# Same-chunk tables of a state-space layer, expanded in DRAM before they are loaded

## The chip, the core and the metric

The kernel runs on one core of one Trainium2 chip. The metric is the device time of one execution in microseconds (us), the median of the runs. The core has TensorE (PE, with its weight loads as PEld), VectorE (DVE), ScalarE (ACT), GpSimd (POOL) and SyncE (SP); 16 DMA engines move data between DRAM and SBUF, for whichever engine issued the transfer.

## What is computed

A trunk of two layers over 256 tokens of 2048 features, all in float32: a convolution module, a feed-forward layer, a state-space module with a gated output, a second feed-forward layer, each added to `x`, and a last norm. The state-space module is the part that the change touches:

```python
u = h.reshape(bsz, L, 128, 16)                  # 128 groups of 16 channels
bu = einsum("blgc,gpc->blgp", u, bb)            # complex, 64 states per group
s = scan(s_t = a * s_{t-1} + bu_t)              # over the 256 tokens
y = Re(einsum("blgp,gcp->blgc", s, c)) + d_skip * h
z = gelu(y) @ w_glu                             # 2048 x 4096
out = z[:, :2048] * sigmoid(z[:, 2048:])
def mlp(h, w_up, w_down):                       # 2048 x 8192 and back
    a = relu(h @ w_up)
    return (a * a) @ w_down
```

## The kernel before

**Stages.** The weights stream from DRAM once, in steps of 1 MB (`raw`, three buffers; the convolution's first steps are smaller). ACT and DVE (for some steps POOL) split every half step into two float32r parts `hi` and `lo` (L117, L119; four buffers each), and PE multiplies them (L194 and L195, L215 to L217). SP issues all loads of `raw` and of the tables in one queue, in program order (`fetch`, L91). The first feed-forward layer is eight slices of `up` and `down`; its last two `down` slices are where the tables of the state-space layer begin to be loaded, by hooks that stand at single steps.

**The state-space layer.** The 256 tokens are cut into 32 chunks of 8. For each block `B` of 32 groups there are three tables of 2 MB, each 128 partitions by 32 groups by 128 floats: `W` takes a chunk's inputs to states (`ssm_front`), `M` takes a chunk's inputs to the outputs of the same chunk (`ssm_local`), `V` takes the state at a chunk's start to its outputs (`ssm_carry`). Between front and carry stand a transposition (`ssm_turn`) and the scan over chunks on DVE (`ssm_scan`, which also reads a 512 KB table `R`); after carry come gelu and the transposed, split output `yT` (`ssm_out`), which the gated product reads. `begin` does blocks 0 and 1 and the front of block 2; the rest is woven into the first eight steps of the gated product by the table `todo`, whose key is the step and its half: the front of block 3 at (1, 1), local of block 2 at (2, 0), its carry and the scan of block 3 at (2, 1), its `ssm_out` at (3, 0), local and carry of block 3 at (3, 1) and (5, 0). Steps 0 and 1 read `yT` of block 0, steps 2 and 3 of block 1, and so on.

**Where the tables come from.** They are computed in the background of the convolution's output product and of the first feed-forward layer: `ssm_prep` fills a list of pieces with a cost each, and `pop_bg` works them off at 2.75 units for each half step. `vstage(k)`, k = 0 to 15, makes `V` for eight groups and writes it to DRAM as `Vd`; `kstage(k)` multiplies it with the input matrix and writes a band of 16 by 15 blocks for each group as `Kd` (64 DMAs of 16 KB, POOL queue). Rows of `M` are shifted windows of that band: the rows of token d within the chunk (16 partitions) are columns 16 d to 16 d + 127 of it. So `table("M", B)` reads `Kd` with eight DMAs, one for each d, each into 16 partitions, in pieces of 128 floats (512 bytes); `W`, `V` and `R` are read with 128 partitions at a time, 8 KB to the row (4 KB for `R`).

**Order.** SP's queue is the program's order: `M` of block 0 is fetched ahead of a `raw` of the first feed-forward layer, `M` of block 1 in `begin`, `M` and `V` of blocks 2 and 3 ahead of the loads of steps 4 and 6 (`before_load`), with `R` of block 3 ahead of step 5. A table waits for a free one of six 16 KB buffers (`blk`). On PE, ACT, DVE and POOL a scheduler sets the order when the program is built.

Of the kernel before, what the change touches and what calls it, by code (L numbers as in the profile page):

```python
# [9 lines left out]
F32 = mybir.dt.float32  # L10
# [8 lines left out]
P = 128  # L19
# [8 lines left out]
G, ST, GC = 128, 64, 16  # L28
CH = 8
VW = PAD + T + 2  # L30
NQ = 4
# [5 lines left out]
class Trunk:  # L37
# [41 lines left out]
    def add(self, view, shape, consume, pre=None):  # L79
        self.steps.append((view, shape, consume, pre))  # L80
# [743 lines left out]
    def ssm_prep(self):  # L824
        nc, a, bg = self.nc, self.a, self.bg
        add = lambda c, fn: bg.append((c, fn))
        const = self.const
        self.Wd = self.dram.tile([P, G, P], F32, name="Wd")
        self.Kd = self.dram.tile([G, GC, 15 * GC], F32, name="Kd")
        self.Vd = self.dram.tile([P, G, P], F32, name="Vd")  # L830
        self.Bd = self.dram.tile([G, 2, ST, GC], F32, name="Bd")
        self.Rd = self.dram.tile([P, NQ, 1024], F32, name="Rd")
        self.xs = self.dram.tile([T, D], F32, name="xs")
        dma = nc.gpsimd.dma_start
# [221 lines left out]
        def vstage(k):  # L1056
            vs = s["bv"][:, 1, 0:1152].rearrange("p (g d c) -> p g d c", d=9, c=GC)
            g = slice(8 * k, 8 * k + 8)
            c = [s["c12"][:, i, g, :].unsqueeze(2).broadcast_to([P, 8, 8, GC]) for i in range(2)]
            p = [s[x][:, g, :].unsqueeze(3).broadcast_to([P, 8, 8, GC]) for x in ("pr", "pi")]  # L1060
            t = self.t4([P, 8, 8, GC], name="vt")
            v = vs[:, :, 1:9, :]
            self.tt(v, c[0], p[0], ALU.mult)
            self.tt(t, c[1], p[1], ALU.mult)
            self.tt(v, v, t, ALU.add)
            nc.scalar.activation(vs[:, :, 0, :], s["c12"][:, 0, g, :], AF.Copy)
            dma(out=self.Vd[:, g, :], in_=v.rearrange("p g d c -> p g (d c)"))

        def kstage(k):
            vs = s["bv"][:, 1, 0:1152].rearrange("p (g x) -> p g x", x=9 * GC)  # L1070
            bs = s["bv"].rearrange("p i x -> p (i x)")
            ps = self.bank([P, 2, P], name="kp")
            for gl in range(8):
                q, hh = gl % 4, gl // 4
                nc.tensor.matmul(ps[32 * q:32 * q + 32, hh, :], lhsT=bs[:, (8 * k + gl) * GC:(8 * k + gl + 2) * GC],
                                 rhs=vs[:, gl, 0:P], start=hh == 0, stop=hh == 1, skip_group_check=True)
            ks = self.t2([P, 2, P], name="ks")
            nc.scalar.activation(ks, ps, AF.Copy)
            for j in range(2):
                self.stt(ks[:, j, 0:GC], self.m32[:, 0:GC], self.dgl[:, k, j:j + 1], ks[:, j, 0:GC], ALU.mult, ALU.add)  # L1080
            kd = self.Kd.rearrange("(k h q) c e -> k q c h e", k=16, h=2, q=4)
            for q in range(NQ):
                dma(out=kd[k, q, :, :, 7 * GC:15 * GC], in_=ks[32 * q:32 * q + GC])
        for k in range(16):
            add(12, lambda k=k: vstage(k))
            add(5, lambda k=k: kstage(k))


    def ssm_slice(self, n):
# [46 lines left out]
    def table(self, kind, B):  # L1136

        if kind == "R":
            t = self.t4([P, 2, 16, 32], name="R") if B != 2 else self.S[:, 1]
            self.fetch(t.rearrange("p i g j -> p (i g j)"), self.Rd[:, B])  # L1140
        else:
            t = self.blk_tile([P, 32, P], name=kind + "t")
        if kind in "WV":
            src = self.Wd if kind == "W" else self.Vd
            for h in range(0, 32, 16):
                self.fetch(t[:, h:h + 16, :], src[:, 32 * B + h:32 * B + h + 16, :])
        elif kind == "M":
            base = self.Kd[32 * B:32 * B + 32]
            for d in range(CH):
                self.fetch(t[d * GC:(d + 1) * GC], base[:, :, d * GC:d * GC + P].rearrange("g c x -> c g x"))  # L1150
        self.tables[kind, B] = t

    def ssm_block(self, b):
# [306 lines left out]
```

## Time and profile before

| | us |
|---|---|
| median of 3 runs | 2077.03 (2071.52 to 2077.48) |
| profiled execution, its own time | 2073.18 |
| its span, first to last instruction | 2071.4 |
| PE busy | 1996.2 (96%) |
| DVE busy | 1426.4 (69%) |
| ACT busy | 942.6 (46%) |
| POOL busy | 304.4 (15%) |
| `Mt<-Kd`, 32 DMAs of 256 KB, median to landing | 14.1 |
| `Wt<-Wd`, 8 DMAs of 1 MB, median to landing | 9.8 |
| `Vt<-Vd`, 8 DMAs of 1 MB, median to landing | 12.3 |

[...] Times in rows are counted from the span's start. The state-space layer lies at about 1083 to 1206 us, the first feed-forward layer ahead of it, the second behind it.

### The profile page before, as it was taken

The page shows a single profiled execution, that of the slowest core. Times are in us where ns is not written, and L with a number is a line of the kernel's source. Part 1 is how long each engine was busy: PE and PEld are TensorE (multiplying, and loading weights), DVE is VectorE, ACT ScalarE, POOL GpSimd, SP SyncE. Part 2 cuts the span into 40 slices and gives each one's busy share as a digit, 9 for nine tenths or more (in the row PEclk, how much of TensorE's full clock was granted, in tenths as well). Part 3 has the DMA queues.
Part 4 walks back from the last instruction along what each step waited for, and adds up shares of the span by engine and source line. Part 5 has one row for each costly group of instructions (what it writes and reads, how often), then busy time and mean ns, then how long its engine had stood idle before and what let it go on. Part 6 is the DMA issues. An engine that isn't in the chain of part 4 may idle for free.

```text
span 2071.4 us, 28883 instructions
## 1 busy us (share of the span) xinstructions
PE 1996.2 (96%) x11612; PEld 1696.8 (82%) x11612; DVE 1426.4 (69%) x1897; ACT 942.6 (46%) x1155; POOL 304.4 (15%) x234
## 2 busy tenths in 40 slices
PE   8999798999999999999987799999999999999998
PEld 8899587788888888888876588888888888888887
DVE  7999899966767777776548635566565555655555
ACT  5444454454444545444433244455344444544444
POOL 2987401100000211111013410000000000000000
PEclk9999999999999999999997999999999999999999
DMA  8667367766856876667999975666566566565663
GB/s 230 164 176 209 108 201 246 229 216 189 266 185 188 220 217 214 202 213 225 254 299 222 216 234 184 192 184 193 184 189 197 183 189 197 183 211 192 186 192 133
DMA packets 330485, 420.09 MB, mean 203 GB/s; under 512 B 10081, under 2 KB 228241, under 8 KB 327889
## 3 DMA queue, kind: packets, MB, share of 16 engines
q1 hardware_dynamic: 316864, 384.86, 62.8%
q0 software_dynamic: 9488, 29.02, 4.7%
q10 hardware_dynamic: 4000, 4.38, 0.7%
q8 instruction: 91, 1.49, 0.3%
q14 instruction: 42, 0.34, 0.0%
HBM read 391.69 MB, written 26.53 MB: 202 GB/s over the span
## 4 chain that ended last, share of the span: by engine, by line
PE 79%; DVE 12%; DMA 4%; SPq 1%; issue 1%; ACT 1%; POOL 1%; ACTq 0%; POOLq 0%; DVEq 0%
PE acc L194 22%; PE acc L215 14%; PE acc L216 14%; PE acc L217 14%; PE acc L195 11%; DVE cv L792 6%; DMA raw<-in_ssm_w_glu_dram 2%; DVE lo L119 1%; SPq L91 1%; DVE vT L426 1%; DVE ws L783 1%; DMA raw<-in_mlp_w_down_dram 1%; DMA Vt<-Vd 0%; PE acc L204 0%; PE acc L205 0%
## 5 line engine op out<-in xcount | busy, mean ns | idle before, releaser
L117 ACT ACTIVATE hi<-raw 128x1024 fp32r<-128x1024 f32 x672 | 711.0, 1060 | 983.7 <-PE acc L217 480.0
L119 DVE TENSOR_TENSOR lo<-raw,hi 128x1024 fp32r<-128x1024 f32 x596 | 729.3, 1224 | 534.5 <-ACT hi L117 533.5
L194 PE MATMUL acc<-hT,hi 128*128 128x512 f32 x2048 | 726.5, 399 | 3.4 <-DVE t L771 3.4
L195 PE MATMUL acc<-hT,lo 128*128 128x256 f32 x2048 | 575.3, 281 | 3.3 <-DVE lo L119 3.3
L194 PEld LDWEIGHTS acc<-hT,hi 128*128 128x128 f32 x2048 | 385.3, 188 | 100.0 <-issue 3.2
L215 PE MATMUL acc<-hi,rT 128*128 128x512 f32 x992 | 388.6, 392 | 6.2 <-ACT hi L117 6.2
L195 PEld LDWEIGHTS acc<-hT,lo 128*128 128x128 f32 x2048 | 387.5, 189 | 4.8 <-DVE lo L119 3.9
L216 PE MATMUL acc<-lo,rT 128*128 128x512 f32 x992 | 387.4, 391 | 0.5 <-DVE lo L119 0.5
L217 PE MATMUL acc<-hi,rT 128*128 128x512 f32 x992 | 387.0, 390 | 0.0
L215 PEld LDWEIGHTS acc<-hi,rT 128*128 128x128 f32 x992 | 186.8, 188 | 47.2 <-ACT hi L117 6.6
L217 PEld LDWEIGHTS acc<-hi,rT 128*128 128x128 f32 x992 | 186.8, 188 | 39.5
L216 PEld LDWEIGHTS acc<-lo,rT 128*128 128x128 f32 x992 | 186.7, 188 | 39.0 <-DVE lo L119 1.0
L119 POOL TENSOR_TENSOR lo<-raw,hi 128x1024 fp32r<-128x1024 f32 x76 | 187.3, 2482 | 115.4 <-ACT hi L117 106.6
L204 PE MATMUL acc<-hT,hi 128*128 128x256 f32 x512 | 146.0, 285 | 1.5 <-ACT hi L117 1.5
L206 PE MATMUL acc<-hT,lo 128*128 128x256 f32 x512 | 145.4, 284 | 1.9 <-POOL lo L119 1.9
L205 PE MATMUL acc<-hT,hi 128*128 128x256 f32 x512 | 146.1, 286 | 0.2 <-DVE hT L252 0.2
L792 DVE SCALAR_TENSOR_TENSOR cv<-vT,dw,cv 128x256 f32<-128x256 f32 x348 | 142.1, 478 | 0.8
L217 PE MATMUL acc<-hi,yT 128*128 128x512 f32 x256 | 101.3, 396 | 8.1 <-DVE yT L231 8.1
L783 DVE TENSOR_TENSOR x<-x,acc 128x1024 f32<-128x1024 f32 (+1 forms) x72 | 83.6, 1161 | 33.3 <-PE acc L217 22.9
L204 PEld LDWEIGHTS acc<-hT,hi 128*128 128x128 f32 x512 | 98.5, 192 | 4.1 <-ACT hi L117 2.1
L215 PE MATMUL acc<-hi,yT 128*128 128x512 f32 x256 | 101.6, 397 | 0.0
L206 PEld LDWEIGHTS acc<-hT,lo 128*128 128x128 f32 x512 | 98.5, 192 | 3.0 <-POOL lo L119 2.1
(264 smaller groups left out, 1759.1 us busy)
## 6 DMA issues: line engine op xcount, KB each, us to landing
raw<-in_mlp_w_up_dram SPq DMA_DIRECT2D x128, 1024.0 KB, 5.8
raw<-in_mlp_w_down_dram SPq DMA_DIRECT2D x128, 1024.0 KB, 5.2
raw<-in_ssm_w_glu_dram SPq DMA_DIRECT2D x32, 1024.0 KB, 5.6
raw<-in_conv_w_in_dram SPq DMA_DIRECT2D x60, 512.0 KB, 5.5
raw<-in_conv_w_out_dram SPq DMA_DIRECT2D x16, 1024.0 KB, 5.3
Vd<-bv POOLq DMA_DIRECT2D x16, 512.0 KB, 5.0
Wt<-Wd SPq DMA_DIRECT2D x8, 1024.0 KB, 9.8
Mt<-Kd SPq DMA_DIRECT2D x32, 256.0 KB, 14.1
```

What stands on the lines that cost most here:

```text
L117: self.nc.scalar.activation(hi, sl, AF.Copy)
L119: ins = eng.tensor_tensor(out=lo, in0=sl, in1=hi.bitcast(F32), op=ALU.subtract)
L194: mm(accs[m], lhsT=hi[:, kk, c], rhs=x, start=first and kk == 0, stop=False)
L195: mm(accs[m][:, 0:T], lhsT=lo[:, kk, c], rhs=x[:, 0, :], start=False, stop=last and kk == 3)
L204: mm(accs[m], lhsT=hi[:, kk, c], rhs=x[:, 0, :], start=first and kk == 0, stop=False)
L205: mm(accs[m], lhsT=hi[:, kk, c], rhs=x[:, 1, :], start=False, stop=False)
L206: mm(accs[m], lhsT=lo[:, kk, c], rhs=x[:, 0, :], start=False, stop=last and kk == 3)
L215: mm(acc[:, b, :], lhsT=ak[:, 0, t], rhs=hi[:, kk, :], start=first and kk == 0, stop=False)
L216: mm(acc[:, b, :], lhsT=ak[:, 0, t], rhs=lo[:, kk, :], start=False, stop=False)
L217: self.mm_last = mm(acc[:, b, :], lhsT=ak[:, 1, t], rhs=hi[:, kk, :], start=False, stop=last and kk == 1)
L783: self.nc.vector.tensor_tensor(out=out, in0=a, in1=b, op=op)
L792: return self.nc.vector.scalar_tensor_tensor(out=out, in0=a, scalar=s, in1=b, op0=op0, op1=op1)
```

## The change

A DRAM tensor `Md` of the shape of `Wd` and `Vd` is added. Thirty-two DMAs on POOL's queue copy the windows of `Kd` into it, DRAM to DRAM, 256 KB each (`mstage(B, d)`: 16 by 32 pieces of 512 bytes). They are listed behind `kstage`, from k = 4 on, for the block that is then complete. To hold the list's pace, `kstage` is entered at 4 and later 3 units instead of 5, an `mstage` at 0.5. `table("M", B)` then reads `Md` as `W` and `V` are read: two DMAs of 1 MB, 128 partitions, 8 KB to the row.

```diff
+        self.Md = self.dram.tile([P, G, P], F32, name="Md")
...
+        def mstage(B, d):
+            dma(out=self.Md[d * GC:(d + 1) * GC, 32 * B:32 * B + 32, :],
+                in_=self.Kd[32 * B:32 * B + 32, :, d * GC:d * GC + P].rearrange("g c x -> c g x"))
         for k in range(16):
             add(12, lambda k=k: vstage(k))
-            add(5, lambda k=k: kstage(k))
+            add(4 if k < 4 else 3, lambda k=k: kstage(k))
+            if k >= 4:
+                for d in range(2 * (k % 4), 2 * (k % 4) + 2):
+                    add(0.5, lambda B=k // 4 - 1, d=d: mstage(B, d))
+        for d in range(CH):
+            add(0.5, lambda d=d: mstage(NQ - 1, d))
...
-        if kind in "WV":
-            src = self.Wd if kind == "W" else self.Vd
+            src = {"W": self.Wd, "M": self.Md, "V": self.Vd}[kind]
             for h in range(0, 32, 16):
                 self.fetch(t[:, h:h + 16, :], src[:, 32 * B + h:32 * B + h + 16, :])
-        elif kind == "M":
-            base = self.Kd[32 * B:32 * B + 32]
-            for d in range(CH):
-                self.fetch(t[d * GC:(d + 1) * GC], base[:, :, d * GC:d * GC + P].rearrange("g c x -> c g x"))
```

SP's queue from the end of the first feed-forward layer to step 6 of the gated product (`raw` are weights, `xJ` the layer's input, the other names the tables), as one piece of the difference:

```order
 L91 DMA Wt<-Wd 128x2048 x2
 L91 DMA xJ<-xs 32x8x128 x4
-L91 DMA Mt<-Kd 16x32x128 x8
+L91 DMA Mt<-Md 128x2048 x2
 L91 DMA Vt<-Vd 128x2048 x2
 L91 DMA Wt<-Wd 128x2048 x2
 L91 DMA raw<-in_ssm_w_glu_dram 128x4x512
-L91 DMA Mt<-Kd 16x32x128 x8
+L91 DMA Mt<-Md 128x2048 x2
 L91 DMA Vt<-Vd 128x2048 x2
 L91 DMA raw<-in_ssm_w_glu_dram 128x4x512
 L91 DMA R<-Rd 128x1024
```

No transfer changes its place; each group of eight `M` loads is two, and `V`, `raw` and `R` stand behind them as before.

POOL's queue around k = 3 to 5 before (`bv` is `vstage`'s result, `ks` that of one `kstage`):

```order
L1083 DMA Kd_2991<-ks_7140 16x2x128 x4
L1067 DMA Vd_2992<-bv_6554 128x8x128
L1083 DMA Kd_2991<-ks_7301 16x2x128 x4
L1067 DMA Vd_2992<-bv_6554 128x8x128 x2
L1083 DMA Kd_2991<-ks_7469 16x2x128 x4
```

and the same place of the changed kernel:

```order
L1084 DMA Kd_2991<-ks_7124 16x2x128 x4
L1068 DMA Vd_2993<-bv_6555 128x8x128
L1087 DMA Md_2992<-Kd_2991 16x32x128 x8
L1084 DMA Kd_2991<-ks_7282 16x2x128 x4
L1068 DMA Vd_2993<-bv_6555 128x8x128
L1084 DMA Kd_2991<-ks_7421 16x2x128 x4
```

The eight copies of a block, which the list has in pairs, stand in one burst ahead of the `Kd` writes of k = 4, 8 and 12, and those of the last block behind k = 15. The first of each burst waits for the `Kd` writes of the step just ahead of it.

## Rows read from the trace of the kernel before

**Rows 1.** The chain that ended last, shares of the span by engine.
```profile
PE 79%; DVE 12%; DMA 4%; SPq 1%; issue 1%; ACT 1%; POOL 1%; ACTq 0%; POOLq 0%; DVEq 0%
```

**Rows 2.** By stretch: window, length; PE, PEld, DVE, ACT, POOL; clock; DMA share, GB/s.
```profile
750.00:800.00 50.00, 50.00 (x304) 41.92 (x303) 36.95 (x40) 22.96 (x29) 7.69 (x13) 1.00 0.73 222
1000.00:1030.00 30.00, 30.00 (x134) 24.82 (x134) 17.58 (x16) 12.12 (x12) 0.00 (x0) 1.00 1.05 332
1045.00:1060.00 15.00, 8.91 (x27) 6.81 (x28) 7.39 (x7) 5.47 (x6) 0.00 (x0) 0.77 1.03 393
1105.00:1135.00 30.00, 18.00 (x254) 15.04 (x258) 29.74 (x28) 8.58 (x12) 12.82 (x6) 0.66 1.16 195
1160.00:1205.00 45.00, 33.96 (x375) 26.77 (x368) 18.32 (x16) 11.26 (x16) 14.24 (x6) 0.90 1.06 270
```

**Rows 3.** SP's timeline, 980 to 1240 us: start, duration, instruction, count.
```profile
1020.10 13.61 SPq L91 DMA_DIRECT2D Mt<-Kd  x8
1033.81 8.59 SPq L91 DMA_DIRECT2D raw<-in_mlp_w_down_dram  x3
...
1105.85 17.77 SPq L91 DMA_DIRECT2D Mt<-Kd  x8
```

**Rows 4.** DMA view, 998 to 1020 us; then 1020 to 1047 us in 40 slices.
```profile
DMA packets 2529, 8.11 MB, mean 369 GB/s; under 512 B 112, under 2 KB 112, under 8 KB 2016
...
GB/s 340 185 264 376 385 388 278 98 98 101 118 102 96 106 115 99 96 112 114 96 99 113 106 95 106 116 99 97 108 134 89 94 127 115 103 112 209 303 366 376
```

**Rows 5.** The weights' transfers issued at 700 to 1000, 1002 to 1020, 1033 to 1042 us.
```profile
DMA to landing us min/median/max: 5.0/5.8/9.8
...
DMA to landing us min/median/max: 5.7/7.5/8.5
...
DMA to landing us min/median/max: 15.6/15.9/16.2
```

**Rows 6.** PE's timeline: start, duration, instruction, count, idle before it and its end.
```profile
1050.62 0.79 PE L215 MATMUL acc<-hi,rT 128*128 128x512 f32 x1 [6.22 <-ACT hi L117]
...
1128.45 1.04 PE L1287 MATMUL yt<-ident,y 128*128 128x128 f32 x8
1133.82 3.64 PE L1262 MATMUL acc<-Mt,xJ 128*32 128x128 f32 x64 [4.34 <-DMA Vt<-Vd]
...
1141.68 1.96 PE L1275 MATMUL acc<-Vt,SS 128*32 128x128 f32 x64
...
1157.89 2.73 PE L1200 MATMUL xw<-Wt,xJ 128*32 128x128 f32 x64 [4.29 <-DVE xJ L1187]
...
1165.83 0.66 PE L1213 MATMUL xtr<-ident,X 128*128 128x128 f32 x4
```

**Rows 7.** Who waited for whom on PE, 1030 to 1215 us: total, times, longest.
```profile
PE acc L217 <- DVE yT L231: 8.1, 1, 8.1
...
PE mv L1275 <- DMA Vt<-Vd: 1.5, 1, 1.5
```

**Rows 8.** DVE's timeline, 1083 to 1212 us, columns as in rows 6.
```profile
1135.23 0.69 DVE L1247 TENSOR_TENSOR SS<-S 64x512 f32<-64x512 f32 x1
...
1141.82 2.36 DVE L783 TENSOR_TENSOR S<-S 128x1024 f32<-128x1024 f32 x2
...
1151.48 2.88 DVE L783 TENSOR_TENSOR SS<-S 64x512 f32<-64x512 f32 x1
...
1173.70 2.41 DVE L783 TENSOR_TENSOR S<-R,xtr 128x496 f32<-128x496 f32 x4 [14.67 <-DMA R<-Rd]
...
1188.12 1.27 DVE L231 TENSOR_TENSOR yT<-yt,yT 128x512 fp32r<-128x512 f32 x2
```

**Rows 9.** POOL: issues of one tile (ns min/median/max, first and last start); timeline.
```profile
L850 POOL DMA_DIRECT2D Kd<-zero x4: 750/758/813, 262.6 to 264.9; - x4
...
783.77 2.02 POOL L1083 DMA_DIRECT2D Kd<-ks  x4 [14.26 <-issue]
...
1151.42 2.39 POOL L119 TENSOR_TENSOR lo<-raw,hi 128x1024 fp32r<-128x1024 f32 x1 [1.19 <-ACT hi L117]
```

## The prediction

> **What bounds the kernel now.** I read the chain of waits first: 79% of it is PE, 4% are transfers and 1% is SP's queue [rows 1]. So only stretches where PE waits or runs at the low clock can give time. The table by stretch shows where these are: PE is busy throughout at 750 to 800 and at 1000 to 1030 us, but in the 15 us from 1045 only for 8.91 at clock 0.77, in the 30 us from 1105 for 18.00 at 0.66, and in the 45 us from 1160 for 33.96 at 0.90 [rows 2]. SP's timeline shows what stands ahead of these places: eight `Mt<-Kd` loads, whose issue alone holds the queue for 13.61 and 17.77 us [rows 3]. The DMA view says why: while they move, about 100 GB/s arrive; in the 22 us before, with `W` loads and weights, it was 369 GB/s [rows 4], though the engines' share shows no idle time in either case (1.16 from 1105, 1.05 from 1000) [rows 2]. Whatever stands behind an `M` load lands late: the weights behind the first one 15.9 us after their issue instead of 5.8 [rows 5].
>
> **Removed and added on SP.** 32 DMAs of 256 KB go, eight of 1 MB come, for the same 8 MB. Per table of 2.1 MB that is 21 us at 100 GB/s, or 5.7 us at 369 [rows 4]. I take 5.7, since the new load has the shape of the `W` loads that make up half of that stretch. So each of the four tables frees some 15 us of transfer. What this is worth I read place by place, since PE needs it only where it waits.
>
> [...] In the rows, pieces of 512 bytes going to 16 partitions arrive at 100 GB/s [rows 4]. [...]
>
> **Place A, `M` of block 0.** The three weights behind it leave SP only from 1033.81 on and land 16 us later; PE stops for 6.22 us and restarts at the low clock [rows 3, 5, 6]. At full speed a matmul takes 30.00/134 = 0.224 us, so the 27 matmuls of the 15 us from 1045 are worth 6 us [rows 2]: 9 us are lost. With two 1 MB loads this place looks like 1000 to 1030, where `W` loads pass among the weights: these land in 5.7 to 8.5 us and PE never stops [rows 2, 5]. Gain 9 us; bounds 7 (the idle time alone) and 10.
>
> **Place B, blocks 1 to 3.** Here I walk along PE and ask at each wait what is late next.
> - *Local of block 1* starts at 1133.82 and takes 3.64 us, where carry, as many matmuls, takes 1.96; PE had finished `yt` at 1129.5 [rows 6]. Its `M`, issued from 1105.85 [rows 3], lands before 1124 if 2.1 MB take 5.7 us, even behind `W` and `xJ`. Local then ends at 1131.5. Carry of block 1 needs the scan's result, which DVE finishes at 1135.9 whatever the loads do [rows 8]. So carry starts there and not at 1141.7: 5.8 us earlier.
> - *The front of block 3* starts at 1157.89 after 4.29 us of waiting for DVE [rows 6], and DVE is what is late next: the scan of block 2 begins at 1135.9 as before. Its main part took until 1144.2; the four `SS` pieces behind it cost 0.69 us each alone, but up to 2.88 while POOL makes a `lo` [rows 8, 9]. With `yT` between them (1.3) the front can start between 1149 and 1157. I take 1153.5, in the middle: of the 5.8 us 4.4 are left.
> - *Carry of block 2* waits 1.5 us for its `V` [rows 7]. `M` of block 2 takes the buffer that local of block 1 frees (1131.5), `V` the one that carry frees (1138); at 5.7 us each, with a weight between, both land by 1146. The wait goes: 5.9 us.
> - *The scan of block 3* waits 14.67 us for `R`, which is queued behind `M` and `V` of block 2; `yT` of block 2 stands behind that scan on DVE, is done at 1189.4, and PE waits 8.1 us for it [rows 7, 8]. Now `R` lands near 1150. The scan then starts when the front is transposed, 1166.5 - 4.4 = 1162 [rows 6]. It held DVE for 14.4 us (1173.7 to 1188.1) under POOL's `lo`; block 2's took 8.3 without [rows 8]; I take 12, and 1.3 for `yT`: 1175.3. PE arrives at 1189.4 - 8.1 - 5.9 = 1175.4. So the wait is gone: 14 us earlier, and with it a restart at the low clock, worth some 1.7 us as in local of block 1.
> - `M` and `V` of block 3 take buffers that are free by 1161 and land by 1170, ahead of their use behind 1180.
>
> Sum for B 16 us; bounds 9 (every DVE piece at its slow value) and 22 (none).
>
> **Added on POOL, 32 copies in four bursts.** An issue of the nearest kind, 224 KB in 512 pieces (`Kd<-zero`), takes 0.76 us, so a burst holds POOL for 6 us, behind up to 5 us of waiting for the `Kd` writes of the step ahead. Queued behind it are the next step's `Kd` writes; POOL idles 14.26 us before those [rows 9], which covers the 11. If that cover were gone, `ks` would be held longer, and the temporaries of the squared ReLU share its three buffers: some 3 us in each of three bursts. How long a copy moves the trace can't show, since it has none from DRAM to DRAM. Bounds: 5.7 us of all engines for a burst at 369 GB/s, 21 at 100 [rows 4]. I take a value near the first, as no side of the copy is 16 partitions of SBUF. It runs beside weights where the engines' share is 0.73 [rows 2]; weights that land in up to 9.8 us stop nothing there, those that leave late and land after 15.6 do [rows 2, 5, 6]. Cost taken as 0, bounds 0 and 8 us; I see nothing in it that could gain. The lower units for `kstage` end the background 12 units, some 4 half steps, sooner; nobody waits for that end. The first `M` is read at 1020, 200 us behind its copies; the others leave more.
>
> **Sum.** 9 + 16 = 25 us off the profiled execution's 2073.18 (its span of 2071.4 and 1.8 around it) gives 2048. The median of the runs stands 3.9 us above that execution, the lowest run 1.7 below it, so I forecast 2050.
>
> **Rivals.**
> - *DVE keeps most of B.* If POOL's `lo` falls on every scan piece, B gives 5 and A 9: 2061. For it: DVE is busy 29.74 of 30 us from 1105 [rows 2]. Against it: the two longest waits in B end with a transfer.
> - *More comes free.* `xs`, `xJ` and `W` of block 2 use the same engines; if they too land sooner, another 10 us go: 2040. Against it: DVE, not a load, is late at the carry of block 0.
> - *The rows arrive no faster.* `W` and `V` take 9.8 and 12.3 us to land. If that is their own speed and not the queue ahead of them, only SP's issue time is saved, 0 to 4 us: 2074. Against it: 369 GB/s [rows 4]. [...]
> - *Slower: the bursts stop PE.* If a copy moves at the 100 GB/s of `Mt<-Kd` and holds all engines for 21 us, each burst is another place A: 4 x 9 = 36 lost against 25, 2085. It decides from where weights land 15 us after issue. Against it: the copies have a queue of their own, so no weight stands behind them in order.
>
> **How the numbers follow.** The forecast has 0.60, DVE's rival 0.17, the larger gain 0.12, no faster rows 0.06, slower 0.05. The range, 2038 to 2066, takes in the first three, with up to 8 us for the bursts, and leaves some 0.13 out. A measurement of this kernel tells about 0.3%, 6 us, from no change. Faster by more than that 0.88, within it 0.07, slower 0.05.
>
> **What would show it.** Right: two `Mt<-Md` issues, under 1 us together, where SP needed 13 to 18; no idle PE at 1044; local of block 1 right behind `yt`; no wait of a scan for `R`; weights landing within 12 us during the copies. Wrong: idle PE between 770 and 1000, an `Mt<-Md` that lands after more than 12 us, or the 8.1 us wait for `yT` still there.

## The result, and the profile after

The changed kernel takes 2048.24 us (median of 4 runs, 2047.30 to 2051.67); the kernel before, run beside it, 2074.28 (4 runs). The ratio over these runs is 0.9881, 95% interval [0.9858, 0.9905]: 25 us, or 1.2%, faster (26 by the two medians), where 2050 was forecast with a range of 2038 to 2066. The profiled execution has a span of 2045.3 us, 26.1 less than before.

The chain that ended last, of the changed kernel:

```profile
PE 84%; DVE 12%; issue 2%; POOL 1%; DMA 1%; ACT 0%; SPq 0%; ACTq 0%; POOLq 0%; DVEq 0%
```

Transfers went from 4% to 1% of it [rows 1]; DVE stayed at 12%. The table by stretch of the changed kernel (window, length; PE, PEld, DVE, ACT, POOL; clock, the granted one of TensorE as a share of full speed; DMA share, GB/s), the same windows as in [rows 2], in which stages from place A on now stand up to 26 us earlier:

```profile
750.00:800.00 50.00, 50.00 (x305) 41.89 (x304) 38.08 (x43) 23.12 (x30) 13.80 (x23) 1.00 0.86 269
1000.00:1030.00 30.00, 30.00 (x134) 24.82 (x134) 17.57 (x16) 11.68 (x11) 0.00 (x0) 1.00 1.01 393
1045.00:1060.00 15.00, 15.00 (x68) 12.43 (x67) 8.48 (x7) 6.69 (x10) 2.31 (x4) 1.00 0.94 286
1105.00:1135.00 30.00, 25.95 (x288) 21.56 (x289) 29.72 (x30) 9.31 (x15) 11.44 (x6) 0.89 0.86 340
1160.00:1205.00 45.00, 45.00 (x314) 36.50 (x313) 21.81 (x21) 22.89 (x30) 16.95 (x7) 1.00 0.58 184
```

Place A (third row) is full at clock 1.00, where it was 0.77: 68 matmuls where there were 27. DVE is as full as before in the fourth row (29.72 of 30), and in the last one PE is busy throughout (45.00 us, where it was 33.96), while the DMA engines' share fell from 1.06 to 0.58. At 750 to 800, where a burst of copies lies, PE loses nothing, though POOL does twice as much.

SP's timeline of the changed kernel at the two loads of [rows 3], and the DMA view of the 10 us in which the first one moves:

```profile
1019.64 0.93 SPq L91 DMA_DIRECT2D Mt<-Md  x2
...
1094.40 1.59 SPq L91 DMA_DIRECT2D Mt<-Md  x2
```

```profile
DMA packets 1201, 3.90 MB, mean 390 GB/s; under 512 B 64, under 2 KB 64, under 8 KB 945
```

0.93 and 1.59 us of issue stand where 13.61 and 17.77 stood, and 390 GB/s (a weight moves in these 10 us too) where it was about 100 [rows 4]. The weights issued between 1019 and 1042 us, one just ahead of the first `M` and four behind it, land 5.2 to 7.6 us after their issue, where it was 15.9 [rows 5]:

```profile
DMA to landing us min/median/max: 5.2/6.1/7.6
```

Who waited for whom on PE, 1030 to 1215 us, in the changed kernel (total, times, longest), all but one of 0.2 us:

```profile
PE xw L1205 <- DVE xJ L1192: 7.4, 1, 7.4
PE xw L1205 <- DMA Wt<-Wd: 4.6, 1, 4.6
PE acc L1280 <- DVE SS L1252: 3.7, 2, 2.7
PE warm L184 <- ACT X L1208: 1.3, 1, 1.3
```

The 8.1 us for `yT`, the 6.2 us at place A and the waits for `V` of [rows 6, 7] are gone. What is left waits mostly for DVE, and one of these waits, the front of block 3, grew from 4.29 to 7.40. PE's timeline of the changed kernel (start, duration, instruction, count, idle before it and its end):

```profile
1116.21 1.48 PE L1292 MATMUL yt<-ident,y 128*128 128x128 f32 x8
1117.62 1.96 PE L1267 MATMUL acc<-Mt,xJ 128*32 128x128 f32 x64
1123.67 1.95 PE L1280 MATMUL acc<-Vt,SS 128*32 128x128 f32 x64
...
1142.99 3.64 PE L1205 MATMUL xw<-Wt,xJ 128*32 128x128 f32 x64 [7.40 <-DVE xJ L1192]
...
1177.62 1.03 PE L1292 MATMUL yt<-ident,y 128*128 128x128 f32 x8
```

Local of block 1 stands right behind `yt` and takes 1.96 us instead of 3.64; the last `yt` comes 26.0 us earlier than before (1203.65).

### The profile page after: what moved, and what is told of

Its sections match the earlier page's. It is cut to its first block, busy times and chain, and to the rows that moved or that the text cites. A ratio compares the mean times of both kernels' runs of the same rounds, so it can differ in the third digit from the quotient of the medians.

```text
span 2045.3 us, 28886 instructions
## 1 busy us (share of the span) xinstructions
PE 1991.8 (97%) x11612; PEld 1695.5 (83%) x11612; DVE 1426.7 (70%) x1897; ACT 943.5 (46%) x1155; POOL 325.9 (16%) x266
## 4 chain that ended last, share of the span: by engine, by line
PE 84%; DVE 12%; issue 2%; POOL 1%; DMA 1%; ACT 0%; SPq 0%; ACTq 0%; POOLq 0%; DVEq 0%
PE acc L194 23%; PE acc L215 15%; PE acc L217 14%; PE acc L216 14%; PE acc L195 11%; DVE cv L792 4%; PE acc L205 1%; PE acc L206 1%; PE acc L204 1%; DVE lo L119 1%; DVE S L783 1%; DVE vT L426 1%; DVE ws L783 1%; DMA raw<-in_conv_w_in_dram 0%; DVE wt L783 0%
## 5 line engine op out<-in xcount | busy, mean ns | idle before, releaser
L117 ACT ACTIVATE hi<-raw 128x1024 fp32r<-128x1024 f32 x672 | 711.5, 1060 | 960.0 <-PE acc L217 501.6
```

Source lines behind the costliest of these rows:

```text
L117: self.nc.scalar.activation(hi, sl, AF.Copy)
```

## Experiments

The kernel before was run beside every one of these; its medians were 2072 to 2075, so kernels of different groups are compared by their ratio to it. The changed kernel stands at 0.9881.

### The copies alone

The 32 copies are made as in the changed kernel, but `M` is loaded from `Kd` as before; `Md` is not read.

```diff
+            if kind == "M":
+                base = self.Kd[32 * B:32 * B + 32]
+                for d in range(CH):
+                    self.fetch(t[d * GC:(d + 1) * GC], base[:, :, d * GC:d * GC + P].rearrange("g c x -> c g x"))
...
```

> The 32 copies of Kd into Md are made with the lower kstage units, as in the change, but M is loaded from Kd as before the change; Md is read by nobody. If the copies are hidden, as the prediction took them, the time stays at that of the kernel before, 2074 us within 6, with PE never idle between 770 and 1000 us. If the bursts hold up the weights, it is 2080 to 2110, with PE idle behind the bursts. M of block 0 still stops PE for some 6 us near 1044.

Measured: 2073.96 us, ratio 0.9996 [0.9979, 1.0012]. The two longest waits on PE that the change removes are still there (8.1 and 6.2 us before), and so is the one at local of block 1 (6.8 us, where it was 4.3):

```profile
PE acc L217 <- DVE yT L231: 7.8, 1, 7.8
...
PE acc L215 <- ACT hi L117: 4.7, 1, 4.7
```

So the copies cost nothing that can be measured within the interval, some 3.5 us to either side, and bring nothing by themselves.

### Block 0 alone, blocks 1 to 3 alone

Both make all copies. One loads only `M` of block 0 from `Md`, the other (with `B == 0` in the condition below) only those of blocks 1 to 3; the rest come from `Kd`.

```diff
+            if kind == "M" and B > 0:
+                base = self.Kd[32 * B:32 * B + 32]
+                for d in range(CH):
+                    self.fetch(t[d * GC:(d + 1) * GC], base[:, :, d * GC:d * GC + P].rearrange("g c x -> c g x"))
...
```

> Only M of block 0 is loaded from Md; M of blocks 1 to 3 comes from Kd as before. By the prediction place A alone is worth 9 us (7 to 10): 2065. If the gain were in the shorter issue alone, without faster arrival, weights would still land 16 us after issue here and the time would stay at 2074. If place A's gain is given back later, because the same three loads still fill the queue behind it, the time also stays above 2070.

> Only M of blocks 1 to 3 is loaded from Md; M of block 0 comes from Kd as before and PE stops for some 6 us near 1044. By the prediction place B alone is worth 16 us (9 to 22): 2058. If A and B add up to the 26 us measured for both, and A is 10, this one is at 2058 too; if they share part of the gain, it is nearer to 2050.

Measured: block 0 alone 2063.30, ratio 0.9943 [0.9915, 0.9971], so 12 us off; blocks 1 to 3 alone 2059.92, ratio 0.9929 [0.9904, 0.9954], 15 us off. Both are near what was expected (2065 and 2058). Together they are 26.5 us, against the 25 of the whole change: the two places add up as far as the intervals tell, which are 5 to 6 us to either side. The split is known better from the traces (below). Waits on PE with block 0 alone:

```profile
PE acc L217 <- DVE yT L231: 4.8, 1, 4.8
PE acc L1273 <- DMA Mt<-Kd: 2.9, 1, 2.9
```

and with blocks 1 to 3 alone:

```profile
PE xw L1211 <- DVE xJ L1198: 7.4, 1, 7.4
PE acc L215 <- ACT hi L117: 4.9, 1, 4.9
```

Each kernel keeps the waits of the place that it leaves. The 7.4 us for `xJ` comes with blocks 1 to 3.

### Why `M` was slow: few partitions, or short pieces

The change does two things to the loads: each reaches 128 partitions instead of 16, and its rows are 8 KB instead of 512 bytes. Two kernels do one each. The first loads `Md` with eight DMAs of 16 partitions, in rows of 16 KB:

```diff
+            if kind == "M":
+                for d in range(CH):
+                    r = slice(d * GC, (d + 1) * GC)
+                    self.fetch(t[r], self.Md[r, 32 * B:32 * B + 32, :])
...
```

> M is loaded from Md, in rows of 16 KB, but with eight transfers of 16 partitions each, as from Kd before. If the rate follows the number of partitions that a transfer fills, M still arrives at about 100 GB/s, SP needs 13 us or more for eight issues in a full queue, and the time is that of before, 2070 to 2077. If it follows the length of the contiguous piece, M arrives at some 370 GB/s and the time is 2046 to 2052.

The second pads each row of `Md` in DRAM, so that 128 partitions are reached at a time, but in pieces of 512 bytes:

```diff
-        self.Md = self.dram.tile([P, G, P], F32, name="Md")
+        self.Md = self.dram.tile([P, G, P + GC], F32, name="Md")
...
-                self.fetch(t[:, h:h + 16, :], src[:, 32 * B + h:32 * B + h + 16, :])
+                self.fetch(t[:, h:h + 16, :], src[:, 32 * B + h:32 * B + h + 16, 0:P])
```

> Each 128-float row of Md is padded in DRAM to 144 floats, so the loads of M reach 128 partitions at a time as in the changed kernel, but in pieces of 512 bytes instead of 8 KB rows. With 16 partitions, 8 to 16 KB rows gave about 2062 (e4_part16) and 512-byte pieces about 2074. Theory partitions decide: the loads still land in about 6 us each, time 2047 to 2053. Theory length decides: M lands at little over 100 GB/s, the places A and B stall again, 2066 to 2074. Both limits multiply: about 1.5 times the landing time of the changed kernel, 2050 to 2056.

Measured: 16 partitions with long rows 2062.03, ratio 0.9933 [0.9911, 0.9955], between what both theories said; 128 partitions with short pieces 2051.14, ratio 0.9905 [0.9887, 0.9922], which overlaps the changed kernel's interval. The DMA views of stretches in which only `M` of block 0 moves, in this order: the kernel before (1027 to 1038 us), 16 partitions with long rows (1028 to 1038), 128 partitions with short pieces (1028 to 1032), the changed kernel (1024.6 to 1027):

```profile
DMA packets 2326, 1.15 MB, mean 105 GB/s; under 512 B 71, under 2 KB 2326, under 8 KB 2326
```

```profile
DMA packets 160, 1.31 MB, mean 131 GB/s; under 512 B 80, under 2 KB 80, under 8 KB 80
```

```profile
DMA packets 2282, 1.16 MB, mean 290 GB/s; under 512 B 16, under 2 KB 2282, under 8 KB 2282
```

```profile
DMA packets 141, 1.02 MB, mean 427 GB/s; under 512 B 16, under 2 KB 16, under 8 KB 16
```

105 GB/s with both faults, 131 with only the few partitions, 290 with only the short pieces, 427 with neither. So most of the rate comes from the 128 partitions; longer rows gave a quarter more on 16 partitions and half again as much on 128.

The time does not follow the rate: by the ratios, 128 partitions alone give 20 of the 25 us and long rows alone give 14, so the two overlap. A quarter more rate, with SP held for 8.38 us by the eight issues and not 13.61, already brings the weights behind `M` some 3.5 us sooner, and PE's stop at place A falls from 6.2 to 2.7 us. Short pieces on 128 partitions cost a third of the rate, but only 5 us of time, within the intervals.

The number of transfers goes with the partitions here (eight of 256 KB against two of 1 MB) and was not varied by itself; size alone is unlikely to be the fault, since the copies, also 256 KB each, land 0.85 us apart (below).

The 105 GB/s are not one fixed rate of such loads: in block 3 of the kernel before, the same short pieces into 16 partitions moved at 139 GB/s from 1178 to 1187 us.

### How many copies are free

Each copy is made four times (and in a later kernel, with `range(1)` below, twice); the further tensors are written and never read.

```diff
+        self.Mx = [self.dram.tile([P, G, P], F32, name=f"Mx{i}") for i in range(3)]
...
-            dma(out=self.Md[d * GC:(d + 1) * GC, 32 * B:32 * B + 32, :],
-                in_=self.Kd[32 * B:32 * B + 32, :, d * GC:d * GC + P].rearrange("g c x -> c g x"))
+            for to in (self.Md, *self.Mx):
+                dma(out=to[d * GC:(d + 1) * GC, 32 * B:32 * B + 32, :],
+                    in_=self.Kd[32 * B:32 * B + 32, :, d * GC:d * GC + P].rearrange("g c x -> c g x"))
```

> Each of the 32 copies is made four times, into Md and into three further DRAM tensors that nothing reads; the loads of M are those of the changed kernel. 25 MB more are read and written in four bursts, each four times as long (about 28 us of transfer and 20 us of issue on POOL). Theory the bursts are hidden because no weight is queued behind them: weights land later, up to some 15 us, PE stops little, 2048 to 2058. Rival the bursts stop PE from where weights land 15 us after issue: each burst costs about 9 us, 2075 to 2090, with idle PE behind 766, 836, 901 and 970.

> Each of the 32 copies is made twice, into Md and into one further DRAM tensor that nothing reads; with one copy each the time was 2048, with four 2074. Theory there is a point from which PE stops, because three raw buffers and four hi and lo buffers cover late weights: weights land up to about 14 us after issue, PE stops nowhere between 760 and 1060, 2047 to 2051. Rival that the loss goes with the volume from the start: a third of the 26 us, 2055 to 2059.

Measured: four times 2074.28, ratio 1.0014 [0.9998, 1.0030], all of the gain lost; twice 2051.00, ratio 0.9894 [0.9860, 0.9927], not to be told from one copy. The interval of the second is wide and does not exclude the near end of its rival (2055); that there is a point, between two and four copies, is read from PE's waits below. The issue-to-landing times of the weights between 700 and 1000 us, for one, two and four copies in this order:

```profile
DMA to landing us min/median/max: 5.0/6.4/12.9
```

```profile
DMA to landing us min/median/max: 5.0/6.8/17.8
```

```profile
DMA to landing us min/median/max: 5.0/7.1/19.9
```

With one and with two copies PE waits for nothing between 700 and 1062 us; with four (total, times, longest):

```profile
PE acc L215 <- ACT hi L117: 3.6, 1, 3.6
PE acc L194 <- DVE t L771: 2.0, 1, 2.0
PE kp L1077 <- DVE bv L783: 1.8, 2, 1.2
PE acc L195 <- DVE lo L119: 1.6, 3, 0.8
```

These and two of 0.8 are 10.6 us, a wait of 3.3 for POOL's `xr` follows, and PE runs at clock 0.93 from 980 to 1005 us and at 0.89 from 1030 to 1060, worth some 5 us more, an estimate from these two clocks. That is 19 of the 22.6 us by which the state-space layer starts later (its first transposition at 1093.3 against 1070.8). Of the 10.6 us, 6.0 are waits for `hi` and `lo`, which is for weights; the other 4.6 are for `t`, `bv` and `ks`. The prediction had a price for these too: `ks` held longer while POOL issues copies. Four copies also hold POOL four times as long (0.63 us an issue, as with one), and how the loss splits between the two causes was not tried. The landing time alone does not decide: in the first of the fourfold bursts three weights in a row land 17.8 to 19.1 us after issue, and PE stays busy from 760 to 860 us; the weights fetched ahead would explain it. The stops come in the later bursts, the largest where the last one runs beside the loads of `W` and `M` of block 0. The weights issued at 1000 to 1030 us in this kernel:

```profile
DMA to landing us min/median/max: 11.6/21.7/22.6
```

At how many bytes, between two copies and four, PE begins to stop is not settled. Where the weights and the copies meet is at the DMA engines. The DMA view with one copy each, 767 to 782 us (queue, packets, MB, share of 16 engines; `q1` carries SP's loads, `q0` POOL's copies):

```profile
DMA packets 3070, 4.84 MB, mean 323 GB/s; under 512 B 174, under 2 KB 2464, under 8 KB 3069
...
q1 hardware_dynamic: 2320, 2.35, 51.0%
q0 software_dynamic: 749, 2.48, 50.5%
```

The two queues share the time of the 16 engines about half and half here, 51.0% and 50.5%, and weights land in up to 12.9 us, where the kernel before had 9.8 [rows 5]: the copies' own queue was no way round the engines.

### What DVE still holds

In the changed kernel the longest wait is for DVE. Two kernels go at it. The first writes the scaling of block 3 (`ssm_scale(3)`, for which PE waits 7.40 us) ahead of the scan of block 2; the second makes the `lo` parts of the gated product's first eight steps (sixteen of them; the expectation counts six) on DVE, not on POOL.

```diff
             self.ssm_scan(1)
+            self.ssm_scale(3)
             self.ssm_carry(1)
...
         def front3():
-            self.ssm_scale(3)
```

```diff
-                    if n == 0:
-                        self.pool_lo.add(len(self.steps))
```

> The scaling of the layer input of block 3 (DVE's xJ, for which the front of block 3 waits 7.40 us in the changed kernel) is written in begin, ahead of the scan of block 2, instead of behind it. Theory DVE's order is what is late next: the 7.40 us go, the scan of block 2 starts about 1 us later, 2041 to 2046. Rival: the scheduler or the loads put another wait there (the carry of block 2 then waits for the scan, which has moved back), 2046 to 2052.

> The second split part lo of the first half steps of the gated product is made by DVE and not by POOL, so no POOL operation lies beside the scan. Theory POOL's lo slows the scan pieces on DVE (0.69 us alone, up to 2.88 beside a lo): the scans get shorter by about as much as DVE's added lo costs or more, 2042 to 2049. Rival DVE is full at that place and each added lo (about 1 us each, six of them) stands ahead of the scan: 2050 to 2058.

> Both edits together: the scaling of block 3 written in begin, ahead of the scan of block 2, and the gated product's first lo parts made by DVE. With lo on DVE alone PE still waits 2.85 us for the scaling. Theory the two add as far as a wait is left: about 2 to 3 us below the 2035 of lo on DVE alone, 2031 to 2034. Rival: the scaling ahead of the scan only moves the scan back, 2034 to 2038.

Measured: the scaling 2045.54, ratio 0.9874 [0.9859, 0.9889], whose interval holds the changed kernel's ratio; `lo` on DVE 2035.26, ratio 0.9825 [0.9809, 0.9841], 12 us better than the changed kernel and below both expectations; both 2035.90, ratio 0.9822 [0.9792, 0.9852], no better than `lo` alone. The wait at the front of block 3 went in the first, but three of 0.8 to 1.8 us for `yT` came: PE now reaches sooner what DVE makes beside and behind the same scan. With `lo` on DVE the wait is 2.9:

```profile
PE xw L1205 <- DVE xJ L1192: 2.9, 1, 2.9
```

The reason can be read in two timelines. In the changed kernel, DVE in the scan of block 2, and POOL beside it (its last line lies beside the scan of block 3):

```profile
1123.47 2.42 DVE L783 TENSOR_TENSOR S<-S,xtr 128x496 f32<-128x496 f32 x4
...
1130.78 6.57 DVE L783 TENSOR_TENSOR S<-S 128x1024 f32<-128x1024 f32 x2
...
1142.24 1.29 DVE L1192 TENSOR_TENSOR xJ<-xJ,rJ 128x512 f32<-128x512 f32 x2
```

```profile
1129.82 3.13 POOL L119 TENSOR_TENSOR lo<-raw,hi 128x1024 fp32r<-128x1024 f32 x1 [2.44 <-ACT hi L117]
1133.42 6.13 POOL L119 TENSOR_TENSOR lo<-raw,hi 128x1024 fp32r<-128x1024 f32 x2 [0.47 <-ACT hi L117]
1150.94 2.38 POOL L119 TENSOR_TENSOR lo<-raw,hi 128x1024 fp32r<-128x1024 f32 x1 [11.39 <-ACT hi L117]
```

and DVE in the same scan with `lo` on DVE:

```profile
1127.93 2.36 DVE L783 TENSOR_TENSOR S<-S 128x1024 f32<-128x1024 f32 x2
1130.20 1.22 DVE L119 TENSOR_TENSOR lo<-raw,hi 128x1024 fp32r<-128x1024 f32 x1
...
1134.75 1.29 DVE L1192 TENSOR_TENSOR xJ<-xJ,rJ 128x512 f32<-128x512 f32 x2
```

Two products of the scan take 6.57 us beside POOL's `lo` and 2.36 without, while a `lo` takes 1.22 us on DVE and some 3 on POOL. Beside the `lo` of the same scan (four, the first at 1124.98), two `S<-S` of 128x496 took 2.70 us (1125.80; 1.25 without, at 1113.61), and an `SS` piece 2.22 (1137.88; 0.69 without). So the four cost DVE some 7.2 us there, an estimate by the sum of these differences, and four `lo` take 4.9 on DVE: here moving a `lo` to DVE costs it less than leaving it on POOL does. These products have both inputs in SBUF; by what means a `lo` slows them was not shown. The four `S<-R,xtr` at 1151.12, whose `xtr` lies in PSUM, did not grow beside the last `lo` above: 2.41 us, as at 1111.28, where no `lo` runs.

### The same edit without the change

`lo` on DVE in the kernel before, with `M` loaded from `Kd` and no copies; the edit is the second of the two diffs above.

> The kernel before (M loaded from Kd, no copies) with the gated product's first lo parts made by DVE instead of POOL. In the changed kernel this edit gave about 12 us. Theory the two edits are independent: before less 12, 2058 to 2062. Rival that the slow M loads hide most of it, since scan, V and R are late anyway there and DVE's shorter scans are followed by a wait for a transfer: less than 6 us, 2066 to 2074.

Measured: 2083.01, ratio 1.0046 [1.0028, 1.0065]: 10 us slower than before, outside of both expectations. PE's timeline of this kernel:

```profile
1130.05 3.21 PE L1262 MATMUL acc<-Mt,xJ 128*32 128x128 f32 x56 [6.36 <-DMA Vt<-Vd]
...
1162.62 1.07 PE L1262 MATMUL mv<-Mt,xJ 128*32 128x128 f32 x12 [7.31 <-issue]
...
1193.38 3.23 PE L1262 MATMUL mv<-Mt,xJ 128*32 128x128 f32 x64 [16.72 <-DMA Vt<-Vd]
```

All three are local products, and the last piece of their `M` lands just ahead of them (at 1129.81, 1162.20 and 1193.29 us; for two of them the view names the `V` behind it, which lands later). DVE is earlier here, so PE reaches the locals sooner, and in the order built with this edit local of block 3 stands ahead of most products of its step. In the kernel before it stood behind them, at 1195.18 us, and PE had work until its `M` was there (1192.96). With `M` loaded from `Kd` (139 GB/s in block 3 of the kernel before) the earlier place is a wait of 16.72 us. So the edit gains 12 us with the changed loads and loses 10 without: in the kernel before, `M` was the bound behind DVE. How much of the loss is the order alone was not tried; nor was a load of `M` into 128 partitions straight from `Kd`, without copies.

## Why the prediction was right, step by step

The forecast was 25 us off, and 25 were measured (26.1 in span). The steps by the traces, in us gained (B's rows are what is gained from its start up to the place named):

| step | forecast | measured |
|---|---|---|
| before the first `W` load | 0 | 0.5 |
| A, `M` of block 0 | 9 | 9.7 |
| the exchange of `xs` and `xJ` | 0 | 2.3 |
| B: up to carry of block 1 | 5.8 | 5.5 |
| B: left at the front of block 3 | 4.4 | 2.4 |
| B: left at carry of block 2 | 5.9 | 4.4 |
| B: all, at the last `yt` | 16 | 13.5 |
| copies | 0 | 0 |

**The rate** was the step on which all rested, and the row it was taken from held: 390 GB/s against 369 [rows 4]. Both rates have weights in them; `M` alone moved at 427. The rival that rows arrive no faster falls with it.

**Place A** went as forecast: its weights land in 5.2 to 7.6 us and PE never stops, as in the stretch that the prediction took for its pattern.

**Place B** was walked along the right waits, in the right order: local of block 1 right behind `yt`, then the scan as what is late, the wait for `R` gone. One term was mis-sized, the front of block 3. The prediction let the main part of the scan of block 2 keep its 8.2 us and only moved POOL's `lo` about on the pieces behind it. Started 12.5 us earlier, the main part itself lay beside four `lo` and took 13.8 us (1123.47 to 1137.28), while the `SS` pieces became short; 2.4 us were left, where the prediction had taken 4.4, the middle of a wide stretch. From there carry of block 2 gained 4.4 instead of 5.9. This is the rival "DVE keeps most of B" in part: `lo` on DVE shows 12 us that it still holds. At the scan of block 3 the prediction took 12 us under `lo`; it took 8.2, as the front's transposition, not `R`, is now what it waits for, and less `lo` lay beside it. So nothing waits for `yT`:

```profile
1151.12 2.41 DVE L783 TENSOR_TENSOR S<-R,xtr 128x496 f32<-128x496 f32 x4 [6.98 <-PE xtr L1218]
...
1161.06 1.29 DVE L231 TENSOR_TENSOR yT<-yt,yT 128x512 fp32r<-128x512 f32 x2 [1.71 <-ACT yT L230]
```

**The 2.3 us at `xs` and `xJ`** are what the rival "more comes free" would give, which was priced at 10; but that the faster `M` brings them is not shown. PE's wait for `xJ` there, 2.5 us before, is gone in the changed kernel and back at 2.5 in the one with two copies, at 2.4 with short pieces. The rest of the rival did not come: the second half of `W` of block 2 still lands 11 us after its issue (PE waits 4.62 us for it, before 3.45), and behind it carry of block 0 waits for DVE, as the prediction held against this rival. That these 2.3 and the 0.5 ahead of the first `W` load made up for what B fell short by is luck, not a step that was right.

**The copies at nothing** were right as a number: an issue took 0.63 us (0.76 taken), and the copies of a burst land some 0.85 us apart, 300 GB/s. Issues of the copies in the changed kernel (ns min/median/max, first and last start), then their landing:

```profile
L1087 POOL DMA_DIRECT2D Md<-Kd x32: 630/630/658, 766.9 to 974.3; - x32
...
DMA to landing us min/median/max: 5.8/8.0/10.1
```

The reason given against the slower rival was not: the copies have a queue of their own, but not engines of their own. What covers them would be that weights are fetched ahead; with two copies each PE waits for nothing between 700 and 1062 us, with four 10.6 us, so the point where the cover ends lies between. The copies were priced near the faster of two rates because no side of them is 16 partitions of SBUF; that it is the partitions that slow `M` no row had shown, and the runs showed 131 GB/s with the few partitions alone, 290 with the short pieces alone and 300 for the copies. The rival's own point, weights landing 15 us after issue, was too low (17.8 with two copies stopped nothing). The mechanism is real: with four copies the gain was lost, in part to weights that land late (6.0 of the 10.6 us).

**The signs** that the prediction named came out as it said but for three, all small. The second pair of `Mt<-Md` issues took 1.59 us, not under 1; weights landed in up to 12.9 us during the copies, not 12; and one `Mt<-Md`, which was to be a sign of being wrong beyond 12 us, landed after 13.5:

```profile
DMA to landing us min/median/max: 4.8/8.9/13.5
```

That one is the second half of `M` of block 1, issued at 1094.93 us behind `W` and `xJ`. It landed at 1108.4, 9 us ahead of its use at 1117.62, so nothing waited for it.

## What to carry to other kernels

Before a table is loaded many times into few partitions, reorder it once in DRAM, while the DMA engines have room to spare (a share of 0.73 here [rows 2], 0.86 with the copies), so that a load reaches all 128 partitions; here that was worth 25 us for 8 MB of copies, and short pieces into 128 partitions would have given 20 of them. Look for the gain where PE waits for what is queued behind the slow load, not at the load. And when transfers stop being the bound, ask again which engine should make what: the same edit on DVE and POOL lost 10 us before the change and gained 12 after it.

## What the runs showed of the hardware

- A load into 16 partitions moved at 105 GB/s in 512-byte pieces and at 131 in 16 KB rows (block 0, nothing else on its way); into 128 partitions at 290 in 512-byte pieces and at 427 in 8 KB rows. Neither the partitions nor the pieces explain the first number alone.
- DRAM-to-DRAM copies of 256 KB in 512-byte pieces, issued by POOL, took 0.63 us of issue and landed 0.85 us apart; from 767 to 782 us their queue had 50.5% of the DMA engines' time and that of SP's loads 51.0%.
- Two float32 products of 128x1024 on DVE took 2.36 us alone and 6.57 beside POOL's `lo`, which took about 3 us each; the same `lo` took 1.22 us on DVE. Four products of 128x496 with one input in PSUM took 2.41 us beside a `lo` and 2.41 without.
